# A hybrid attention layer on one core: the first head group's outputs are split earlier, and the feed-forward's transposes are asked for a quarter sooner

## The chip, the core and the metric

The kernel runs on one core of a Trainium2 chip. The core has five engines with their own instruction streams: TensorE (PE; its weight loads are shown as PEld), VectorE (DVE), ScalarE (ACT), GpSimd (POOL) and SyncE (SP), which here issues all DMAs. Each engine takes its instructions in the order that the built program gives them, and waits on semaphores where an instruction needs another engine's or a DMA's result. The metric is the device time of one execution in microseconds (us), less is better.

## What is computed

One layer of a streaming encoder, for 1024 rows of 1024 numbers in float32, in three parts. Each part's output is RMS-normalised and added to the rows.

```python
h = rmsnorm(x, g_mix_pre);  proj = h @ w_in
y_fox = forgetting_attention(fq, fk, fv, f_logit)          # 8 heads of 64, causal
y_chk = chunked_relpos_attention(cq, ck, cv, rel_bias)     # 8 heads of 64, own chunk + 8 before
y = concatenate([rmsnorm(y_fox, g_fox_out), rmsnorm(y_chk, g_chk_out)])
x = x + rmsnorm(y @ w_out, g_mix_post)
h = rmsnorm(x, g_mem_pre)
y = memory_cross_attention(h, rmsnorm(mem, g_mem_kv), w_mq, w_mk, w_mv, w_mo)   # 4 heads, 256 memory rows
x = x + rmsnorm(y, g_mem_post)
h = rmsnorm(x, g_ff_pre)
y = square(relu(h @ w_ff1)) @ w_ff2
x = x + rmsnorm(y, g_ff_post)
```

## The kernel before

**Numbers in two parts.** Each float32 operand of a product is held as a rounded high part and the rest as a low part (`hi`, `lo`), and a product is three matmuls (`mm3`, lines 102 to 104): high by high, high by low, low by high. A weight tile is loaded into a `wraw` buffer (3 of them, line 87), ACT copies its high part (`whi`, line 96), and DVE or POOL subtracts to get the low part (`wlo`, line 97); there are two buffers each of `whi` and `wlo`. For the weights of the memory, `lo_eng()` picks the engine: DVE and POOL in turn, or DVE alone while the flag `quiet[0]` is set.

**Buffers.** Most activations live in one pool of 31 equal buffers (`u4`). PSUM has pairs of banks under the tags `mm`, `s`, `tr` and `pv`.

**Stages.** After the projections, `attend` runs the sixteen heads two by two, in the order `("c",0) ("c",1) ("f",0) ("f",1) ("f",2) ("f",3) ("c",2) ("c",3)`; "f" are the forgetting heads, "c" the chunked ones. So the forgetting heads are all done before the last two pairs of chunked ones. Each head's result goes to a DRAM tile `od[k][half]` (line 396). Beside the last heads the memory is normalised and transposed (`mem_turn`), and its keys are made: `mem_side(mT, "w_mk", "km")` gives eight tiles of 24 matmuls (`mkm`), and `fold_keys` multiplies them with `w_mq` in advance (`fk`, sixteen results of twelve matmuls, evacuated into `fks` and stored as `wk`). Then the pool `p1` of attention is closed and `p2` opened in its place.

Next come `gpost` and `gmem` (two gain rows spread over all partitions), `head_outputs` for both halves of the rows and group 0 (the forgetting heads): it loads `od` back into `oin` (line 570), multiplies by the group's gain and splits into `yT_hi` (ACT, line 573) and `yT_lo` (DVE, line 574), and sums the squares into `sq` (lines 577 to 582). `mem_side(mT, "w_mv", "vm")` makes the memory's values, again eight tiles (`mvm`). `mix_out` is the output projection (`yw`); its `head_rstd` turns `sq` into the inverse norms with four one-column matmuls a half (`ssh`, line 589). `close_block` adds the residual row (`xth`, line 670) and norms it.

After the cross attention (`cross`, `ms`), `mem_out` makes its output for each half (`ym`). For the second half it takes a function that it calls after each quarter `kp` of the weights:

```python
def meanwhile(kp):
    if kp in (0, 2):
        turn(y0, 0, h3[0], "h3", PAIRS[kp // 2:kp // 2 + 1])
    second_weights(kp)
```

`turn` transposes two row tiles of the first half for the feed-forward (`tr_h`, line 127, evacuated into `h3T`, lines 140 and 141). The feed-forward follows.

**What sets the order.** Where `tc.manual_schedule()` is open (the value projections at the start, and everything from the second half's last output tiles on) the engines take the instructions as written. Everywhere else, and so in all that the change touches, the build places each instruction by its own reckoning of times, earlier-written work first where both could go. The order is then fixed in the program; on the chip nothing overtakes on an engine.

Of the kernel before, what the change touches and what calls it, by code (L numbers as in the profile page):

```python
# [33 lines left out]
def f(ap):  # L34
    return ap.bitcast(F32)


def layer(tc, out, t):
    nc = tc.nc
    ctx = ExitStack()  # L40
    with ctx:
        build(ctx, tc, nc, out, t)


def build(ctx, tc, nc, out, t):
    def pool(name, bufs=1, space=None, stack=ctx, **kw):
        if space is not None:
            kw["space"] = space
        return stack.enter_context(tc.tile_pool(name=name, bufs=bufs, reuse_waits="tile", **kw))
# [9 lines left out]
    def mm_tile(shape, name, tag="mm"):  # L59
        return psp.tile(shape, F32, tag=tag, bufs=2, name=name)  # L60

    def u4(name, shape, dt=F32R):

        return up.tile(list(shape), dt, tag="u4", bufs=31, name=name)
# [18 lines left out]
    def load_w(src, shape, alloc=None, lo_on=None):  # L83
        n = wcount[0]
        wcount[0] += 1
        raw = wp.tile(shape, F32, tag="wraw", bufs=3, name=f"wraw{n}")
        nc.sync.dma_start(raw, src)
        return split_w(raw, shape, n, alloc, lo_on)
# [11 lines left out]
    def mm3(ps, lh, ll, rh, rl, start, stop, more=False):  # L100

        nc.tensor.matmul(ps, lh, rh, start=start, stop=False, skip_group_check=more)  # L102
        nc.tensor.matmul(ps, lh, rl, start=False, stop=False, skip_group_check=more)  # L103
        nc.tensor.matmul(ps, ll, rh, start=False, stop=stop, skip_group_check=more)  # L104
# [15 lines left out]
    def to_T(xa, xb, act, c0, name, tags=("tr", "tr")):  # L120

        trs = [mm_tile([P, 2, 2, P], f"tr_{name}_{k}", tags[k // 4]) for k in range(0, KC, 2)]

        def turn(k, q):
            xn = (xa, xb)[q]
            for j in range(2):
                nc.tensor.transpose(trs[k // 2][:, j, q, :], xn[:, (k + j) * P:(k + j + 1) * P], ident)

        ahead = tags[0] != tags[1]
        if ahead:  # L130
            for k in range(0, KC, 2):
                turn(k, 0)
        for k in range(0, KC, 2):
            if not ahead:
                turn(k, 0)
            turn(k, 1)
            src = trs[k // 2].rearrange("p a q b -> p a (q b)")
            i, o = k // act.per, k % act.per
            dh = act.h[i][:, o:o + 2, c0:c0 + 256]
            nc.scalar.activation(dh, src, AF.Copy)  # L140
            nc.vector.tensor_sub(act.l[i][:, o:o + 2, c0:c0 + 256], src, f(dh))  # L141
# [32 lines left out]
    p1s = ExitStack()  # L174
# [240 lines left out]
    def mem_turn():  # L415
        mT = Act("mT", NM)
        xs = [raw_tile(f"memn{b}") for b in range(2)]
        for b in range(2):
            nc.sync.dma_start(xs[b], md[b])
        to_T(*xs, mT, 0, "mem")  # L420
        return mT

    flip = [0]
    quiet = [False]

    def lo_eng():
        flip[0] ^= 1
        return nc.vector if flip[0] or quiet[0] else nc.gpsimd

    def row_pair(w, kp, nh):  # L430
        return w[kp * 2 * P:(kp + 1) * 2 * P, nh * HT:(nh + 1) * HT].rearrange(
            "(a p) n -> p a n", p=P)

    def mem_side(mT, src, name):

        act = Act(name, NM)
        for nb in range(KC):
            wh, wl = load_w(t[src][nb], [P, KC, P], lo_on=lo_eng())
            ps = mm_tile([P, NM], f"m{name}{nb}")
            for kc in range(KC):  # L440
                mm3(ps, wh[:, kc, :], wl[:, kc, :], mT.hi(kc), mT.lo(kc), kc == 0, kc == KC - 1)
            nc.scalar.activation(act.hi(nb), ps, AF.Copy)
            nc.vector.tensor_sub(act.lo(nb), ps, f(act.hi(nb)))
        return act

    def fold_keys(km):

        for h in range(4):
            for mh in range(2):
                wh, wl = load_w(row_pair(t["w_mqT"], h, mh), [P, 2, HT], lo_on=lo_eng())  # L450
                for kp in range(2):
                    ps = mm_tile([P, 2, NM], f"fk{h}{mh}{kp}")
                    for a in range(2):
                        c = slice((kp * 2 + a) * P, (kp * 2 + a + 1) * P)
                        for d in range(2):
                            mm3(ps[:, a, :], wh[:, d, c], wl[:, d, c], km.hi(h * 2 + d), km.lo(h * 2 + d),
                                d == 0, d == 1)
                    g = u4(f"fks{h}{mh}{kp}", (P, 2, NM), F32)
                    if kp:
                        nc.vector.tensor_scalar(g, ps, 0.0625, None, op0=ALU.mult)  # L460
                    else:
                        nc.scalar.activation(g, ps, AF.Copy, scale=0.0625)
                    nc.sync.dma_start(kd_d[mh * 2 + kp][h // 2][:, :, h % 2 * NM:(h % 2 + 1) * NM], g)
# [67 lines left out]
    for n, (kind, pr) in enumerate(order):  # L531
# [10 lines left out]
        for a in range(2):  # L542
# [5 lines left out]
            if a == 0 and n == 6:  # L548
                mT = mem_turn()
        ops = nxt  # L550
    fold_keys(mem_side(mT, "w_mk", "km"))
    p1s.close()


    quiet[0] = True
    p2s = ExitStack()
    p2 = pool("p2", stack=p2s)
    p2xs = ExitStack()
    p2x = pool("p2x", stack=p2xs)

    def head_outputs(th, g):

        yh = [u4(f"yT_hi{th}{g}{i}", (P, 2, HT)) for i in range(2)]
        yl = [u4(f"yT_lo{th}{g}{i}", (P, 2, HT)) for i in range(2)]
        sq = u4(f"sq{th}{g}", (P, HT), F32)
        for i in range(2):
            o = u4(f"oin{th}{g}{i}", (P, 2, HT), F32)
            for j in range(2):
                kc = g * 4 + i * 2 + j
                nc.sync.dma_start(o[:, j, :], od[kc][th])  # L570
                gc = gcol[:, kc:kc + 1]
                dh = yh[i][:, j, :]
                nc.scalar.activation(dh, o[:, j, :], AF.Copy, scale=gc)
                nc.vector.scalar_tensor_tensor(yl[i][:, j, :], o[:, j, :], gc, f(dh),
                                               op0=ALU.mult, op1=ALU.subtract)
            if i == 0:
                nc.scalar.activation(sq, o[:, 0, :], AF.Square)
                nc.scalar.activation(o[:, 1, :], o[:, 1, :], AF.Square)
            else:
                nc.scalar.activation(o, o, AF.Square)  # L580
                nc.vector.tensor_add(sq, sq, o[:, 0, :])
            nc.vector.tensor_add(sq, sq, o[:, 1, :])
        return yh, yl, sq

    def head_rstd(th, g, sq):
        rs = small.tile([P, 4], F32, tag="rs4", bufs=4, name=f"rs{th}{g}")
        ps = mm_tile([P, 4], f"ssh{th}{g}", "pv")
        for b in range(4):
            nc.tensor.matmul(ps[:, b:b + 1], sq[:, b * P:(b + 1) * P], o512, start=True, stop=True)
        nc.vector.tensor_scalar(rs, ps, EPS, None, op0=ALU.add)  # L590
        nc.gpsimd.tensor_tensor(rs, rs, mhalf[:, 0:4], op=ALU.pow)
        return rs
# [5 lines left out]
    def y_tiles(nm, th):  # L598
        return ([u4(f"y{nm}{th}{b}", (P, D), F32) for b in range(4)],
                [small.tile([P, 2], F32, tag="ssy", bufs=8, name=f"ss{nm}{th}{b}") for b in range(4)])  # L600

    PAIRS = ((0, 1), (2, 3))
# [76 lines left out]
    def turn(y, th, act, nm, pairs=PAIRS):  # L679
        for a, b in pairs:  # L680
            to_T(y[a], y[b], act, a * P, f"{nm}{th}{a}")
# [38 lines left out]
    gpost = gain(p2, t["g_mix_post"], "g_mix_post")  # L720
    gmem = gain(p2, t["g_mem_pre"], "g_mem_pre")
    h2, h3 = [], []
    parts = {(th, 0): head_outputs(th, 0) for th in range(2)}
    quiet[0] = False
    vm = mem_side(mT, "w_mv", "vm")
    quiet[0] = True
    ys = [y_tiles("w", th) for th in range(2)]
    mix_out((0, 1), 0)
    for th in range(2):
        parts[th, 1] = head_outputs(th, 1)  # L730
# [23 lines left out]
    def second_weights(kp):  # L754
        if kp == 3:
            wo.extend(load_w(vd_d[k][1], [P, 2, HT], u4, lo_eng()) for k in range(4))
# [7 lines left out]
    h3 = [Act("h3T0")]  # L764
    y0, o = y, o1
# [118 lines left out]
    xf, wo = {}, []  # L884

    def meanwhile(kp):
        if kp in (0, 2):
            turn(y0, 0, h3[0], "h3", PAIRS[kp // 2:kp // 2 + 1])
        second_weights(kp)

    mem_out(1, o, y, ss, gmpost, (0,), meanwhile)
    for i in range(4):
        for a in range(2):
# [530 lines left out]
```

## Time and profile before

Three runs took 1562.92, 1563.53 and 1563.54 us; the median is 1563.53.

| | |
|---|---|
| profiled execution, its own time | 1564.92 us |
| its span | 1562.8 us |
| mean granted TensorE clock | 0.988 |
| PE busy | 1502.7 us (96%), 7948 instructions |
| DVE busy | 940.7 us (60%) |
| ACT busy | 795.9 us (51%) |
| POOL busy | 386.6 us (25%) |
| chain that ended last: PE / DVE / issue / ACT / DMA | 82% / 6% / 3% / 3% / 3% |
| DMA | 237.49 MB, mean 152 GB/s |

Shares of the span. A matmul's busy time is longer than the distance to the next, since matmuls overlap, so a busy PE is read together with the starts of its instructions. In a timeline line the columns are start, duration, engine, line, operation, output and inputs; the bracket at its end is the engine's idle time just before and what ended it. A line of SPq is a DMA being issued, not the transfer.

### The profile page before, as it was taken

Reading aid. Unit: us, or ns where it says so; the run is one execution under the profiler, and the core shown is the slowest. Engines: PE = TensorE matmul, PEld = TensorE weight load, DVE = VectorE, ACT = ScalarE, POOL = GpSimd, SP = SyncE. Lnnn points to the kernel's source line nnn. Section 1 sums busy time; section 2 is a strip of 40 time slices with the busy share of each in tenths; the row PEclk is TensorE's granted clock in tenths of the full one; section 3 lists DMA queues with packets and bytes.
Section 4 is the critical chain, followed back from the end, with each engine's and each line's share of the span. In section 5 each row is a group of like instructions: output and inputs, shape, how many; then the busy total and the mean of one; then the engine's idle time right before and its main releaser. Section 6 shows DMA issues by size and latency. Waiting matters only on the chain.

```text
span 1562.8 us, 22218 instructions
## 1 busy us (share of the span) xinstructions
PE 1502.7 (96%) x7948; PEld 1277.9 (82%) x7948; DVE 940.7 (60%) x1608; ACT 795.9 (51%) x1409; POOL 386.6 (25%) x550
## 2 busy tenths in 40 slices
PE   8999999999999967999999989999999999999998
PEld 7978889789878967776888877888888888888886
DVE  6366574755476743368655568666555574846577
ACT  5356564665466744555454345554555444444442
POOL 4234341343233531002220240433323100000011
PEclk9999999999999998999999999999999999999999
DMA  5132231242223483157523453775444495535565
GB/s 212 50 94 65 60 104 32 81 131 64 55 68 102 144 285 113 68 202 269 197 86 114 156 176 114 253 258 197 153 156 148 166 399 203 171 100 194 208 241 190
DMA packets 90640, 237.49 MB, mean 152 GB/s; under 512 B 10505, under 2 KB 18705, under 8 KB 90530
## 3 DMA queue, kind: packets, MB, share of 16 engines
q1 hardware_dynamic: 90530, 236.08, 45.3%
q8 instruction: 63, 1.03, 0.3%
q14 instruction: 47, 0.39, 0.1%
HBM read 168.35 MB, written 59.30 MB: 146 GB/s over the span
## 4 chain that ended last, share of the span: by engine, by line
PE 82%; DVE 6%; issue 3%; ACT 3%; DMA 3%; POOL 2%; SPq 0%; DVEq 0%; POOLq 0%; ACTq 0%
PE fx L103 4%; PE fx L104 3%; PE fx L102 3%; PE fy L102 3%; PE fy L104 3%; PE fy L103 3%; PE px L104 3%; PE px L102 3%; PE px L103 3%; PE v L104 2%; PE v L102 2%; PE v L103 2%; PE ms L104 2%; PE ms L102 2%; PE ms L103 2%
## 5 line engine op out<-in xcount | busy, mean ns | idle before, releaser
L96 ACT ACTIVATE whi<-wraw 128x1024 fp32r<-128x1024 f32 x92 | 96.8, 1057 | 97.8 <-PE ms L104 29.2
L97 DVE TENSOR_TENSOR wlo<-wraw,whi 128x1024 fp32r<-128x1024 f32 x64 | 79.2, 1243 | 78.4 <-ACT whi L96 78.3
L1151 ACT ACTIVATE whif<-ra 128x1024 fp32r<-128x1024 f32 x37 | 39.2, 1060 | 122.5 <-PE fy L103 62.6
L1153 DVE TENSOR_TENSOR wlof<-ra,whif 128x1024 fp32r<-128x1024 f32 x37 | 45.3, 1225 | 91.2 <-ACT whif L1151 91.2
L1267 POOL TENSOR_SCALAR rf<-sf 128x1 f32<-128x1 f32 x8 | 8.3, 1034 | 326.4 <-ACT jf L1252 326.2
L97 POOL TENSOR_TENSOR wlo<-wraw,whi 128x1024 fp32r<-128x1024 f32 x28 | 67.3, 2405 | 63.6 <-ACT whi L96 42.3
L102 PE MATMUL v<-whiv,hT_hi 128*128 128x256 f32 (+1 forms) x256 | 73.2, 286 | 1.5 <-DVE vs L238 1.5
L104 PE MATMUL v<-whiv,hT_lo 128*128 128x256 f32 (+1 forms) x256 | 73.0, 285 | 0.2 <-DVE hT_lo L141 0.2
L103 PE MATMUL v<-wlov,hT_hi 128*128 128x256 f32 (+1 forms) x256 | 73.1, 286 | 0.0
L104 PE MATMUL fx<-vhif,wlof 128*128 128x512 f32 x168 | 65.4, 389 | 0.0
L102 PE MATMUL fx<-vhif,whif 128*128 128x512 f32 x168 | 65.4, 389 | 0.0
L103 PE MATMUL fx<-vlof,whif 128*128 128x512 f32 x168 | 65.4, 389 | 0.0
L1041 POOL TENSOR_TENSOR sc<-wf,wf 128x512 f32<-128x512 f32 x14 | 22.1, 1579 | 143.4 <-DMA wf<-in_w_ff 117.7
L102 PE MATMUL yw<-whi,yT_hi 128*128 128x512 f32 x128 | 50.3, 397 | 3.4 <-ACT yw L626 1.9
L102 PE MATMUL ym<-whi,oT_hi 128*128 128x512 f32 x128 | 49.8, 404 | 3.0 <-DVE h3T_lo L141 3.0
L103 PE MATMUL yw<-wlo,yT_hi 128*128 128x512 f32 x128 | 50.3, 393 | 1.7 <-DVE wlo L97 1.7
L103 PE MATMUL ym<-wlo,oT_hi 128*128 128x512 f32 x128 | 51.1, 399 | 0.0
L104 PE MATMUL ym<-whi,oT_lo 128*128 128x512 f32 x128 | 51.0, 398 | 0.0
L103 PE MATMUL ms<-wlo,h2T_hi 128*128 128x512 f32 x128 | 50.4, 394 | 0.0
L102 PEld LDWEIGHTS v<-whiv,hT_hi 128*128 128x128 f32 x256 | 48.7, 190 | 1.9 <-DVE vs L238 1.7
L104 PE MATMUL yw<-whi,yT_lo 128*128 128x512 f32 x128 | 49.9, 390 | 0.0
L104 PE MATMUL ms<-whi,h2T_lo 128*128 128x512 f32 x128 | 49.9, 394 | 0.0
(752 smaller groups left out, 5160.9 us busy)
## 6 DMA issues: line engine op xcount, KB each, us to landing
ra<-gd SPq DMA_DIRECT2D x56, 512.0 KB, 3.8
wg<-in_w_ff SPq DMA_DIRECT2D x56, 512.0 KB, 5.8
wf<-in_w_ff SPq DMA_DIRECT2D x38, 512.0 KB, 3.8
gd<-s SPq DMA_DIRECT2D x48, 256.0 KB, 2.1
wraw<-in_w_qk SPq DMA_DIRECT2D x16, 512.0 KB, 3.5
wraw<-wk SPq DMA_DIRECT2D x16, 512.0 KB, 3.5
wraw<-wv SPq DMA_DIRECT2D x16, 512.0 KB, 3.5
gd<-u SPq DMA_DIRECT2D x32, 256.0 KB, 2.4
```

The costliest lines, as they stand in the source:

```text
L96: nc.scalar.activation(hi, raw, AF.Copy)
L97: (lo_on or nc.gpsimd).tensor_sub(lo, raw, f(hi))
L102: nc.tensor.matmul(ps, lh, rh, start=start, stop=False, skip_group_check=more)
L103: nc.tensor.matmul(ps, lh, rl, start=False, stop=False, skip_group_check=more)
L104: nc.tensor.matmul(ps, ll, rh, start=False, stop=stop, skip_group_check=more)
L1041: eng.tensor_sub(sc[:, k1], r0[:, k0], r1[:, k0])
L1151: nc.scalar.activation(ah, ra, AF.Copy)
L1153: nc.vector.tensor_sub(al, ra, f(ah))
L1267: nc.gpsimd.tensor_scalar(r, ssf[b][:, 0:1], ssf[b][:, 1:2], EPS, op0=ALU.add, op1=ALU.add)
```

## The change

Three things in the text of the program:

- `head_outputs` and its call for group 0 (`parts`) stand before `fold_keys(mem_side(mT, "w_mk", "km"))`, so ahead of the keys and of the closing of `p1`; they stood after the two gains, ahead of `vm`.
- `quiet[0]` isn't lowered around `vm` any more, so `lo_eng()` gives DVE for all of its eight weight splits; four of them were POOL's.
- `meanwhile` asks for the second pair of transposes after the second quarter of the weights, where it was the third.

The number of matmuls, transfers and bytes is the same.

```diff
         ops = nxt
-    fold_keys(mem_side(mT, "w_mk", "km"))
-    p1s.close()
-
-
-    quiet[0] = True
-    p2s = ExitStack()
-    p2 = pool("p2", stack=p2s)
-    p2xs = ExitStack()
-    p2x = pool("p2x", stack=p2xs)
-
     def head_outputs(th, g):
...
         return yh, yl, sq
+
+    parts = {(th, 0): head_outputs(th, 0) for th in range(2)}
+    fold_keys(mem_side(mT, "w_mk", "km"))
+    p1s.close()
+
+
+    quiet[0] = True
+    p2s = ExitStack()
+    p2 = pool("p2", stack=p2s)
+    p2xs = ExitStack()
+    p2x = pool("p2x", stack=p2xs)
...
     h2, h3 = [], []
-    parts = {(th, 0): head_outputs(th, 0) for th in range(2)}
-    quiet[0] = False
     vm = mem_side(mT, "w_mv", "vm")
-    quiet[0] = True
...
     def meanwhile(kp):
-        if kp in (0, 2):
-            turn(y0, 0, h3[0], "h3", PAIRS[kp // 2:kp // 2 + 1])
+        if kp < 2:
+            turn(y0, 0, h3[0], "h3", PAIRS[kp:kp + 1])
         second_weights(kp)
```

## The prediction

> **What bounds the kernel now.** I read the page first: TensorE (PE) is busy for 96% of the span and carries 82% of the chain that ended last, so the kernel is bound by PE wherever PE has work, and a change pays only where PE waits. Next the chain in order of time, which shows one long wait: from 566 us it leaves PE for the loads of `wraw` and `oin` (11.5 us in one piece) and comes back at about 594. Then a table of stretches, with columns of length and then busy time (with count) of PE, PEld, DVE, ACT and POOL, the granted clock, the DMA share and GB/s:
>
> ```profile
> core 0: us, PE busy (x) PEld busy (x) DVE busy (x) ACT busy (x) POOL busy (x), PEclk, DMA share, GB/s
> 493.70:513.75 20.05, 19.93 (x163) 19.32 (x162) 13.34 (x39) 14.13 (x32) 10.43 (x19) 1.00 0.44 148
> 513.75:567.10 53.35, 53.35 (x445) 53.26 (x445) 38.22 (x94) 37.16 (x73) 24.22 (x43) 1.00 0.60 186
> ...
> 573.75:594.54 20.79, 1.87 (x8) 1.78 (x9) 10.36 (x15) 10.27 (x17) 3.32 (x2) 0.61 0.69 243
> ...
> 567.10:616.20 49.10, 28.79 (x211) 27.89 (x210) 19.64 (x28) 19.74 (x29) 11.99 (x6) 0.79 0.57 186
> ```
>
> The first two rows are the last heads of attention: PE full, ACT and DVE two thirds full. The last is the stage of the memory's values (`vm`, eight tiles of 24 matmuls), and the row above it the hole within it. The timeline says whose hole it is; PE, ACT, then SP's queue:
>
> ```profile
> 573.45 0.28 PE L104 MATMUL mvm<-mT_hi,wlo 128*128 128x256 f32 x1
> 591.41 1.87 PE L589 MATMUL ssh<-o,sq 128*128 128x1 f32 x8 [17.68 <-DVE sq L582]
> 594.54 0.58 PE L102 MATMUL mvm<-mT_hi,whi 128*128 128x256 f32 x1 [1.26 <-DVE vm_lo L443]
> ```
> ```profile
> 586.10 1.39 ACT L573 ACTIVATE yT_hi<-oin,gcol 128x512 fp32r<-128x512 f32 x2 [9.01 <-DMA oin<-od]
> ```
> ```profile
> 568.86 1.28 SPq L570 DMA_DIRECT2D oin<-od  x2
> 570.19 0.47 SPq L179 DMA_DIRECT2D g_mix_post<-in_g_mix_post  x1
> 570.70 0.50 SPq L179 DMA_DIRECT2D g_mem_pre<-in_g_mem_pre  x1
> 571.58 0.33 SPq L670 DMA_DIRECT2D xth<-in_x  x1
> ...
> 574.55 1.23 SPq L570 DMA_DIRECT2D oin<-od  x2
> ```
>
> The small matmuls `ssh` stand in PE's fixed order ahead of the third `mvm` tile. They wait for `sq`, that for ACT, that for `oin`, whose loads left in a burst with two gains, two rows of x and the weights.
>
> **Gain: the hole closes.** I compared the fixed order of instructions that each build gives every engine. In the changed one the eight `oin` loads stand some fifty places earlier in SP's queue, among the loads of `w_mk`, and both `ssh` groups among the fold of the keys; between the eight `mvm` tiles nothing foreign is left. A full-speed `mvm` matmul starts every 0.12 us (573.33 to 573.45), so the stage costs 8 x 24 x 0.12 = 23.0 us, where it took 49.0 (567.11 to the first `yw` at 616.13). The difference contains the hole, 1.9 us of slow clock after it (20 matmuls 0.213 us apart) and some 1.3 us at two tiles split on POOL (2.40 us each). The flag for those splits is not lowered any more, so all go to DVE at 1.23 us; with ACT's 1.06 that is 2.3 us, less than the 2.9 of a tile, and PE hides it.
>
> The two gains and two rows of x now stand before the third `mvm` weight in SP's queue. That weight can be issued about 2 us before the stage starts (its buffer is freed by the last POOL split of the keys) and must land by 3.4 us into it (two tiles, 5.8, less the split). It has 5.4 us; loads of weights in the burst took 5.3 in the median, `xth` 10.0. So a wait of 0 to 4.6 us; I take 0.7, by the row of its own kind. Stage: 23.7, a gain of 25.3. The 8 `ssh` columns, which were inside the 49.0, are now outside: 0.95 us (their row at full clock, 602.29) back.
>
> **Cost: the work moves onto full engines.** What moves is 14 ACT operations (8 `yT_hi`, 6 squares: 10.05 us in their rows) and 14 of DVE (8 `yT_lo`, 5.74 us; 6 additions to `sq`, 0.69 each). The built order puts nearly all of it in the stretch 493.70 to 513.75, and ahead of the evacuation of `mkm0` and `mkm1`. Those two tiles hold both `mm` banks, so `mkm2` cannot start: in before, PE filled this stretch with 94 `mkm` matmuls, of which 22 finish the first pair; the other 72 (8.6 us) now stand after it. PE waits in the stretch and does that work later, where it was full. ACT's load there becomes 14.13 + 9.0 (one square falls later) - 2.8 (two weight splits and two evacuations that go with the 72) = 20.3 us; DVE's 13.34 + 5.74 + 2.8 - 2.1 = 19.8. Both fill a stretch that took 20.05, and they feed each other. How tightly they pack is bounded by rows: in 300 to 305 both are busy 4.9 of 5 us, in 445 to 465 about 0.8. So 20.3/0.97 = 20.9 to 20.3/0.80 = 25.4 us, and I take 0.9, between, 22.5. Loss: 2.5 + 8.6 = 11.1 (9.5 to 14.0). It cannot be nothing unless PE finds other work, and its order has none. What is left over (one square, two additions) hides in the 53.35 us that follow, with ACT at 70%. For thinner cover later and stray idle I add 1.3 (0 to 4).
>
> The eight `oin` issues take SP some 0.62 us each and push five loads of `w_mk`, a bias row and four stores of `od` back, 1.2 us a pair. They hide behind the same closed banks. Ten `u4` buffers are held some 80 us longer; `fks` tiles then reuse one seven stores back, 7 x 1.44 us of fold against a store that lands in 4.0, so no wait.
>
> The Trainium skill, "TensorE: Matmul & The Clock Gate" (Part 1), speaks against the move: an idle window of about 3.4 us puts PE at half rate until it has been busy as long. This trace agrees at 594.54 (0.213 us against 0.12 after the hole). If the stretch's idle came in one such piece it would add an estimated 1.7 us (half of 3.4) and make the time 1553.2; in bits it adds none, and the sum is without it.
>
> **The second edit does nothing.** Moving the second pair of transposes from the third quarter to the second of `mem_out` could end PE's wait before `ym11`:
>
> ```profile
> 910.01 0.66 PE L127 MATMUL tr_h<-ident,ym 128*128 128x128 f32 x4 [0.99 <-DVE h3T_lo L141]
> 913.65 0.80 PE L102 MATMUL ym<-whi,oT_hi 128*128 128x512 f32 x1 [2.98 <-DVE h3T_lo L141]
> ```
>
> That is 4.0 us of idle and 13 matmuls at 0.427 us for 0.227, 2.6 more: 6.6 at most. In the other direction, if PE came to them before the last row is normed (893.6), it would lose some 4. But this region is ordered by a scheduler's own reckoning, and from the last `mvm` on the built order of all five engines is the same, instruction for instruction. So 0: the wait at 913.65 stays.
>
> **Sum.** -25.3 + 0.95 + 11.1 + 1.3 = -12.0 us. The profiled execution took 1564.92 us (span 1562.8, 2.1 around it), 1.4 above the median of 1563.53. 1564.92 - 12.0 = 1552.9, against the median 1551.5. The likeliest case's own range, with the bounds above, is 1548.5 to 1558.
>
> **Rivals.**
> - *The burst takes the place of the hole.* The third weight lands after 10.0 us as `xth` did: 4.6 instead of 0.7, and 1.9 us of slow clock. For it: the DMA share of 1.00 in 567 to 574. Against: the eight `oin` loads (2 MB) are out of the burst. 1551.5 + 3.9 + 1.9 = 1557.3.
> - *ACT stands still under the heads: slower.* ACT takes its work in order, so each `yT_hi` whose load is late stops the attention behind it. The loads come in four pairs, and the order leaves each some 3 us; if they take the 7.7 us that they took in the burst, 4 x 4.7 = 19 us are added: 1570. It decides from 3 us a pair (12.0/4). For: the last pair stands in SP's queue behind a load that waits for a POOL split. Against: the DMA share is 0.44 there, and weights in 485 to 515 landed in 3.5 us.
> - *The moved work hides wholly.* PE finds its 8.6 us under the heads and the packing costs nothing: -25.3 + 0.95, 1539. Against: PE is in order, and `mkm2` waits for the banks.
> - *Gain and cost cancel.* The packing falls to 0.6 (20.3/0.6 = 34 us in place of 22.5): -12.0 + 11.5, 1563. Nothing in the trace is as loose as that.
>
> **How the numbers follow.** Forecast 0.60, burst 0.18, slower 0.10, hidden wholly 0.08, cancelled 0.04. The range, 1544 to 1562, holds the forecast, the burst and what lies between the forecast and full hiding; it leaves out the slower case, the far end of full hiding and the cancelled one. A measurement of this kernel can tell about 0.2% (3.1 us) from no change. Faster by more: 0.60 + 0.08 + 0.15 of the burst's 0.18 = 0.83; within: 0.07; slower: 0.10.
>
> **What would show it.** Right: no `ssh` wait on `sq` over 1 us; the eight `mvm` tiles in about 24 us at clock 1.00; PE idle of 8 to 13 us in the c5 head with ACT or DVE near full, and `mkm2` released by an evacuation; the wait before `ym11` still some 3 us. Wrong: PE still full in that head (the cost is too high), `yT_hi` waiting for `oin` by more than 3 us a pair (too low), a wait over 4 us for `wraw` at the third `mvm` tile, or a changed stretch at 910.

## The result, and the profile after

Five runs each on one chip: before 1563.01 us in the median (1562.63 to 1563.54), after 1554.26 us (1553.09 to 1559.4). The ratio is 0.995, with a 95% interval of 0.9933 to 0.9966: faster by 8.8 us. The profiled execution of after has a span of 1552.2 us against 1562.8, 10.6 less, at a granted clock of 0.993 (0.988).

The table of stretches of after answers to the one shown of before. Its columns are the stretch and its length, then the busy time and count of PE, PEld, DVE, ACT and POOL, the granted clock, the DMA share and GB/s. The three rows are the c5 head, the heads and the fold that follow, and the eight tiles of the values:

```profile
492.99:515.11 22.12, 16.42 (x92) 14.10 (x90) 19.98 (x44) 19.18 (x42) 9.46 (x17) 0.79 0.55 188
515.11:580.10 64.99, 64.13 (x531) 63.84 (x532) 43.03 (x105) 41.44 (x78) 29.05 (x46) 0.99 0.54 166
580.10:606.20 26.10, 23.55 (x194) 23.14 (x193) 12.83 (x16) 10.45 (x15) 0.00 (x0) 1.00 0.74 258
```

The values' stage was 49.0 us and is 26.1. The c5 head was 20.05 us with 163 matmul records, and is 22.12 with 92: the 71 that are missing stand in the second row, which grew from 445 to 531 (the eight `ssh` are in it too). DVE and ACT are busy for 19.98 and 19.18 of 22.12 us. The stage of the values starts 13.0 us later (580.10 for 567.10; this execution was 0.7 us ahead at the first `sc5g`, 465.6 for 466.3), and the first `yw` 9.9 us earlier (606.2 for 616.1).

The timeline of after's PE in the three places, each line with start, duration, engine, line, operation, and in brackets the idle time before it and what ended it:

```profile
501.80 0.36 PE L389 MATMUL pvc5g<-phc5g,vs 128*128 128x256 f32 x1 [1.36 <-ACT phc5g L383]
504.75 0.36 PE L390 MATMUL pvc5g<-plc5g,vs 128*128 128x256 f32 x1 [2.59 <-DVE plc5g L384]
...
515.42 0.57 PE L102 MATMUL mkm<-mT_hi,whi 128*128 128x256 f32 x1 [0.39 <-DVE km_lo L443]
...
587.81 0.39 PE L102 MATMUL mvm<-mT_hi,whi 128*128 128x256 f32 x1 [1.79 <-ACT whi L96]
589.07 0.39 PE L104 MATMUL mvm<-mT_hi,wlo 128*128 128x256 f32 x1 [0.76 <-DVE wlo L97]
```

PE stands in pieces under the c5 head; `mkm2` is let go at 515.42 by an evacuation (`km_lo`). `ssh` has no wait any more. The third tile of the values waits 1.79 + 0.76 us for its weight. What that weight waited for, on ACT and in SP's queue of after:

```profile
586.70 1.06 ACT L96 ACTIVATE whi<-wraw 128x1024 fp32r<-128x1024 f32 x1 [3.14 <-DMA wraw<-in_w_mv]
```
```profile
573.25 0.45 SPq L179 DMA_DIRECT2D g_mix_post<-in_g_mix_post  x1
...
574.37 0.72 SPq L179 DMA_DIRECT2D g_mem_pre<-in_g_mem_pre  x1
575.18 1.07 SPq L671 DMA_DIRECT2D xth<-in_x  x2
576.34 1.50 SPq L463 DMA_DIRECT2D wk<-fks  x2
577.94 1.89 SPq L87 DMA_DIRECT2D wraw<-in_w_mv  x2
```

Its load leaves at 577.94 behind two gains, two rows of x and some stores of `wk`, and ACT can start on it at 586.70, 8.8 us later.

### The profile page after: what moved, and what is told of

Read it like the earlier page. It is cut to its first block, busy times and chain, and to the rows that moved or that the text cites. A ratio compares the mean times of both kernels' runs of the same rounds, so it can differ in the third digit from the quotient of the medians.

```text
span 1552.2 us, 22221 instructions
## 1 busy us (share of the span) xinstructions
PE 1504.1 (97%) x7948; PEld 1276.3 (82%) x7948; DVE 946.2 (61%) x1612; ACT 796.5 (51%) x1409; POOL 379.6 (24%) x546
## 3 DMA queue, kind: packets, MB, share of 16 engines
q8 instruction: 63, 1.03, 0.3%
## 4 chain that ended last, share of the span: by engine, by line
PE 84%; DVE 6%; ACT 3%; DMA 3%; issue 2%; POOL 2%; SPq 0%; DVEq 0%; POOLq 0%; ACTq 0%
PE fx L103 4%; PE fx L104 4%; PE fx L102 3%; PE fy L104 3%; PE fy L103 3%; PE fy L102 3%; PE px L104 3%; PE px L103 3%; PE px L102 3%; PE ms L104 2%; PE ms L103 2%; PE ms L102 2%; PE v L102 2%; PE pz L103 2%; PE pz L104 2%
## 5 line engine op out<-in xcount | busy, mean ns | idle before, releaser
L97 DVE TENSOR_TENSOR wlo<-wraw,whi 128x1024 fp32r<-128x1024 f32 x68 | 84.3, 1244 | 75.0 <-ACT whi L96 74.5
L97 POOL TENSOR_TENSOR wlo<-wraw,whi 128x1024 fp32r<-128x1024 f32 x24 | 58.1, 2422 | 48.0 <-ACT whi L96 26.9
```

What stands on the lines that cost most here:

```text
L97: (lo_on or nc.gpsimd).tensor_sub(lo, raw, f(hi))
```

## The experiments

Each kernel was timed in five rounds beside before on the same chip; ratios are to before, with 95% intervals.

**The second edit alone** (before, with the transposes asked for a quarter sooner).

```diff
-        if kp in (0, 2):
-            turn(y0, 0, h3[0], "h3", PAIRS[kp // 2:kp // 2 + 1])
+        if kp < 2:
+            turn(y0, 0, h3[0], "h3", PAIRS[kp:kp + 1])
```

> The kernel before with the second edit alone (second pair of transposes after the second quarter). Theory: the built order of all engines is that of before, so nothing happens: 1563 us within 1.5, and the wait before ym11 stays 2.98 us. Rival (the edit moves the transposes): that wait and the slow clock behind it shrink, 1556 to 1560.

1563.34 us, ratio 0.9999 (0.999 to 1.0007). PE's line before `ym11` in it has the same wait as before and after:

```profile
911.62 0.55 PE L102 MATMUL ym<-whi,oT_hi 128*128 128x512 f32 x1 [2.98 <-DVE h3T_lo L141]
```

The second edit does nothing; all of the 8.8 us is the first's.

**The first edit without its move** (after, with the group read and split behind the fold of the keys; of the first edit only the splits' engine is left).

```diff
-    parts = {(th, 0): head_outputs(th, 0) for th in range(2)}
     fold_keys(mem_side(mT, "w_mk", "km"))
+    parts = {(th, 0): head_outputs(th, 0) for th in range(2)}
```

> The first edit without its move: the first group's outputs are read and split after the fold of the keys, where they stood, and only the splits of the values' weights go to VectorE instead of GpSimd. Theory (the gain is the hole's, the flag is worth the two POOL splits on the path, 1.3 us): 1562.2 us, 1560 to 1564, with a wait of ssh for sq of 10 us or more between the values' tiles. Rival (GpSimd's splits held up the weights' loads, and the flag closed the hole): 1545 to 1553, no such wait.

1560.99 us, ratio 0.9985 (0.9976 to 0.9994). The hole is there, on PE:

```profile
590.97 1.87 PE L590 MATMUL ssh<-o,sq 128*128 128x1 f32 x8 [16.59 <-DVE sq L572]
```

So the splits' engine gives some 2.3 us (0.9 to 3.8 by the interval), and the move the rest. The group here is written just ahead of the two gains, where before had it behind them; the first `oin` pair leaves ahead of the gains in both.

**The values' splits back on GpSimd, in after.**

```diff
+    quiet[0] = False
     vm = mem_side(mT, "w_mv", "vm")
+    quiet[0] = True
```

> The changed kernel with the splits of the values' weights put back on GpSimd where its turn comes (four of the eight tiles), everything else as changed. Theory (a tile of 2.9 us hides 1.06 of ACT and 1.23 of VectorE but not 1.06 and 2.40 of GpSimd, so each of the four tiles waits 0.5 to 0.65 us): a stage longer by 2.0 to 2.6 us, 1555.5 to 1558 us. Rival 1 (the weights stand early enough that GpSimd hides too): within 0.6 us of the changed kernel. Rival 2 (GpSimd frees the buffers later and the next loads leave later): 4 us or more over the changed kernel, with waits for wraw.

1554.41 us, ratio 0.9947 (0.9934 to 0.9961); after, on the same chip: 1553.68. The waits for POOL's splits appear, but three of 0.43 us (1.3 in all), and the waits for the third weight are 1.03 + 0.76 where they were 2.12 + 0.76 in after's execution on this chip. The stage is 27.4 us where that execution had 26.4, so it is longer by 1.0 and not by the theory's 2.0 or more; the 0.7 between the medians is inside the intervals.

**After once more.**

> The changed kernel once more, unedited, so that the other runs of this row stand beside it on the same chip. If its scatter (1553.1 to 1559.4 in the first result) is its own and not the first chip's: a median of 1553 to 1556, a ratio to before of 0.993 to 0.997, and runs spread over more than 3 us. If the scatter was the chip's: the same median, runs within 1.5 us.

1553.68 us (1552.47 to 1554.55), ratio 0.9937 (0.9923 to 0.995). The runs lay within 2.1 us, between what the two expectations said; the run of 1559.4 in the first result did not come again.

**The keys' tiles ahead of the moved work.** If the closed banks make the loss, opening them first should give it back; if the load of ACT and DVE makes it, nothing should change.

```diff
+    km = mem_side(mT, "w_mk", "km")
     parts = {(th, 0): head_outputs(th, 0) for th in range(2)}
-    fold_keys(mem_side(mT, "w_mk", "km"))
+    fold_keys(km)
```

> The changed kernel with head_outputs written after the eight mkm tiles and ahead of the fold. Theory (most of the cost is PE work shut out by the two closed mm banks): mkm2 is back at its old place, PE is full in the stretch of head c5, the 8.6 us of put-off matmuls and the half clock are gone, and the same ACT and DVE work costs 0 to 3 us later: 1543 to 1548. Rival (the load on ACT and DVE costs the same wherever it lies): 1552 to 1556.

1548.35 us, ratio 0.9904 (0.9891 to 0.9917): 0.35 us above the theory's range, and well clear of the rival. Its stretches:

```profile
500.00:520.00 20.00, 20.00 (x163) 19.60 (x164) 13.19 (x36) 11.78 (x27) 9.06 (x16) 1.00 0.47 153
520.00:550.00 30.00, 26.94 (x204) 24.70 (x203) 28.17 (x64) 28.10 (x55) 15.90 (x22) 1.00 0.61 190
```

PE is full under the c5 head. The same work now stands under the c6 head, where DVE and ACT are busy 28.2 and 28.1 of 30 us, and PE's idle there is 3.1 us in bits under 1 us. The values' stage starts at 574.8 instead of 580.1: of the 13.0 us some 5 came from the closed banks.

**The burst behind the values' tiles, in after.** The two gains are written behind `vm`, and a copy of one column of the last tile into each target makes them and the first two rows of x wait for it.

```diff
+            if nm == "h2" and tb < 2:
+                nc.vector.tensor_copy(xt[:, 0:1], f(vm.hi(7, slice(0, 1))))
             nc.sync.dma_start(xt, xin(tb))
...
+        nc.vector.tensor_copy(g[:, 0:1], f(vm.hi(7, slice(0, 1))))
+        nc.sync.dma_start(g, src.to_broadcast([P, D]))
```

> The changed kernel with the two gains and the first two rows of x loaded only when the last vm tile is done (a one-column copy from it into each destination ahead of its load). Theory (the third mvm weight was late because 2 MB stood ahead of it): no wait for wraw at mvm2, the stage of eight tiles 23.5 instead of 26.1 us, 1551 to 1553. Rival (it was late by its own issue): stage 26, 1554; or the late rows of x make close_block wait, above 1555.

1551.48 us, ratio 0.9923 (0.991 to 0.9936). The stage is what 192 matmuls at 0.12 us come to:

```profile
579.30:602.20 22.90, 22.90 (x193) 22.90 (x192) 12.84 (x16) 10.38 (x15) 0.00 (x0) 1.00 0.68 223
```

That the gains' and rows' loads made the third weight late is shown: with them gone from there it leaves 2.2 us ahead of the stage, as in after, lands 4.1 us later, and no `mvm` waits. The stage is 3.2 us shorter. The whole time's gain over after is 2 to 4 us by the ratios, and there the intervals overlap.

**Both placings together.**

> Both better placings in one kernel: the tiles of the keys opened before the moved work, and the two gains and the first two rows of x loaded only behind the last tile of the memory's values. Theory (each edit takes away a wait of its own, and the first has already taken most of the second's: with the keys first the waits for the weight in the values' stage were 1.05 us against 2.55 in the changed kernel): 1547.3 us, 1545.5 to 1548.5, the values' stage 23.0 us. Rival 1 (the gains add up: 5.9 and 2.8 off 1554.3): 1545.6 or less. Rival 2 (the late loads are now the last thing before the first rows are normed, and PE waits there): 1549 or more, with a wait at the first transposes of h2.

1545.9 us, ratio 0.9886 (0.9872 to 0.9899): inside the theory's range, but 1.4 us under its price and 0.3 above rival 1, so that these runs don't tell whether the second edit's gain is the smaller for the first. The values' stage takes 23.2 us (574.1 to 597.3), with no wait in it. Against after on the same chip (1553.68) it is 7.8 us less. It beats both kernels.

**What is left under the c6 head.** On top of both placings: first a kernel that leaves out four squares and six additions, then one that leaves nothing out and issues squares later.

```diff
                 nc.scalar.activation(sq, o[:, 0, :], AF.Square)
+            if g == 0:
+                continue
...
```

> The kernel with keys first and late loads, with four of the six squares of the moved first group (3.38 us of ScalarE by their rows: twice 0.63, twice 1.06) and its six additions (4.1 us of VectorE) left out, so that the norm of the first group is taken from a quarter of its values. What is left of the price of the move there is 2.83 us of PE idle in 520 to 550, where ScalarE is busy 27.50 of 30 us and VectorE 28.64. Theory (PE waits because the two are full): with some 3 to 4 us less work on each, PE's idle there falls under 1 us and the time to 1543 to 1544.5 us. Rival (each wait is the length of a chain from score to weight, whatever the load): 1545.2 to 1546.8 us, idle still over 2 us.

```diff
...
     vm = mem_side(mT, "w_mv", "vm")
+    for th in range(2):
+        early[th][3]()
...
```

> The kernel with keys first and late loads, with the same six squares issued after the values' tiles in the code, nothing left out. The built order lets three of them go ahead under the heads as before and moves two squares of 0.63 us and the sums behind the heads, where ScalarE is half idle. Theory (the load under the c6 head is the price): about half of the 2.83 us of idle goes, 1544 to 1545.3 us. Rival (the order of the rest decides, or the sums are late for ssh): 1545.5 us or more.

1543.77 us, ratio 0.9879 (0.9864 to 0.9894), and 1544.33 us, 0.9879 (0.9862 to 0.9895). The row of 520 to 550, first of the kernel with both placings, then of the one without the squares, then of the one with squares later:

```profile
520.00:550.00 30.00, 27.17 (x206) 24.95 (x205) 28.64 (x67) 27.50 (x55) 16.09 (x23) 1.00 0.60 190
```
```profile
520.00:550.00 30.00, 28.57 (x225) 26.99 (x224) 26.30 (x70) 26.98 (x55) 15.72 (x24) 1.00 0.66 203
```
```profile
520.00:550.00 30.00, 27.73 (x218) 26.23 (x217) 26.99 (x66) 28.42 (x57) 15.04 (x24) 1.00 0.66 205
```

With the work gone idle fell by half, from 2.83 to 1.43 us, not to under 1 as the theory had it and not to over 2 as the rival; 19 more matmul records fit in. With squares issued later it fell only to 2.27, where about half was expected to go. Both times agree with the theories, but their intervals overlap with that of both placings alone, so a price of 1 to 2 us for the load is possible and not settled.

**The wait before `ym11`.** It stayed in after, so its cause was tried: the output tiles that follow use the banks which the late transposes hold. Swapping the two pairs of banks, first in after, then on top of both placings:

```diff
-                tr = mm_tile([P, 2, 2, P], f"trx{a}{kp}", ("tr", "pv")[self.i])
+                tr = mm_tile([P, 2, 2, P], f"trx{a}{kp}", ("pv", "tr")[self.i])
...
-        ps = row_tile(o, b, wo, f"ym11{b}", "tr" if b < 2 else "pv")
+        ps = row_tile(o, b, wo, f"ym11{b}", "pv" if b < 2 else "tr")
```

> The changed kernel with the PSUM tags of the last output tiles exchanged (ym110, ym111 in pv and the other two in tr, and the feed-forward's turns the other way round). Theory (ym110 waits for the tr banks that the second pair of transposes holds until their last subtraction): the 2.98 us wait goes, with most of the slow clock after it, 1548 to 1552. Rival (the next thing, row sums or POOL, is late instead): 1554, with the wait under another name.

> The kernel with keys first and late loads, and the banks of the last output tiles and of the transposes swapped as well. Theory (the wait before ym11 is only moved on, as the swap alone showed): 1545 to 1547 us, the same as without the swap. Rival (the swap alone was masked by a chance wait for a weight in the values' stage): 1540 to 1543.5 us.

1555.36 us, ratio 0.9944 (0.9932 to 0.9957), against after's 0.995 and 0.9937; and 1544.38 us, 0.9883 (0.9868 to 0.9897), against 0.9886. The wait is gone (the `ym` stage took 91.9 us from first to last start, after 98.6) and nothing is won: the stage of the transposes `trx` behind it took 32.6 us in place of 25.9. PE's groups in the later half of the kernel, first of after, then with the swap alone, show where it went (count, busy and mean ns, then the idle before them):

```profile
L102 PE MATMUL ym<-whi,oT_hi 128*128 128x512 f32 x128 | 49.6, 402 | 3.0 <-DVE h3T_lo L141 3.0
...
L104 PE MATMUL px<-h3T_hi,wlo_a 128*128 128x512 f32 x24 | 9.6, 401 | 0.6 <-DVE wlo_a L827 0.5
```
```profile
L102 PE MATMUL ym<-whi,oT_hi 128*128 128x512 f32 x128 | 48.5, 394 | 0.0
...
L104 PE MATMUL px<-h3T_hi,wlo_a 128*128 128x512 f32 x24 | 10.6, 441 | 3.1 <-DVE wlo_a L827 3.1
```

PE comes earlier to the feed-forward's first weights and waits there 3.1 us for their split on DVE, where it had waited 0.6. The granted clock of the 8 us behind that wait (950 to 958) was 0.68, so the slow matmuls came back as well.

**All of the keys' splits on VectorE, in after.** PE's longest idle under the c5 head in after, 2.59 us, ended with a DVE operation behind one `yT_lo` of 2.78 us, where the others took 0.73 to 1.09.

```diff
+    quiet[0] = True
     parts = {(th, 0): head_outputs(th, 0) for th in range(2)}
```

> The changed kernel with all sixteen splits of the keys' weights on VectorE, where every second one was GpSimd's; nothing left out. In the changed kernel one yT_lo of VectorE took 2.78 us where its median is 0.75: it began beside a GpSimd split (500.26 to 503.00) and ended 0.55 us after it, and PE's longest idle of the stretch, 2.59 us, ended with what stood behind it. Theory (a VectorE operation that reads two tiles in SBUF stands until GpSimd's is over): no yT_lo of the group over 1.2 us, PE's longest idle in the stretch under 1.5 us; VectorE has 2.0 us less of standing and 1.23 of one more split, so the time falls by 0.5 to 2 us, to 1552 to 1553.5, and less of the stretch is at half clock. Rival 1 (the long yT_lo waits for its own data and GpSimd stands beside it by chance): it stays over 2 us. Rival 2 (the standing goes, but the splits fill VectorE, which sets the stretch): no long yT_lo, and the time at 1554 us or more.

1553.77 us, ratio 0.9952 (0.9938 to 0.9965). Under the heads the theory is right: the longest `yT_lo` is 1.00 us, PE's longest idle in the stretch 1.34, and the values' stage starts at 578.1, 2.0 us earlier than in after. The time is that of rival 2 all the same, no better than after's by the ratio (0.995 and 0.9937), but it came about in another way. The values' stage is now 28.3 us; PE, then ACT:

```profile
585.22 0.39 PE L102 MATMUL mvm<-mT_hi,whi 128*128 128x256 f32 x1 [1.24 <-DVE vm_lo L443]
589.43 0.39 PE L102 MATMUL mvm<-mT_hi,whi 128*128 128x256 f32 x1 [1.08 <-ACT whi L96]
590.69 0.39 PE L104 MATMUL mvm<-mT_hi,wlo 128*128 128x256 f32 x1 [0.76 <-DVE wlo L97]
```
```profile
582.51 1.06 ACT L96 ACTIVATE whi<-wraw 128x1024 fp32r<-128x1024 f32 x1 [3.31 <-DMA wraw<-in_w_mv]
```

PE comes to the stage sooner, and the burst of loads is still there: two weights are waited for instead of one. ACT stood 3.31 us for the third weight before it evacuated the first tile, so the third tile waited for its bank (`vm_lo`), and the fourth tile waited for its own weight. Some 15 matmuls after that start 0.21 us apart. What was won under the heads was lost here.

## Why the prediction came out as it did

It said 1551.5 us, 12.0 less than before; measured were 8.8 (first result) and 10.0 less (after once more), and 10.6 in the spans. The direction and the mechanism were right, and a term of the sum was too good. By the trace the change is worth 9.2 us at the first `yw`: the stage of the values is 22.9 us shorter, for 25.3, and starts 13.7 later, for 13.35.

- *The hole closes.* Right: no `ssh` waits, and nothing foreign stands between the tiles. Undoing the move alone brought back a wait of 16.59 us.
- *The third weight's wait, 0.7 us.* This is the term that was mis-sized, and a row was misread for it. The 5.3 us are the median of this row of before (540 to 600):

```profile
wraw<-in_w_mv SPq DMA_DIRECT2D x7, 512.0 KB, 5.3
```
```profile
572.00 0.82 SPq L87 DMA_DIRECT2D wraw<-in_w_mv  x1
573.73 0.77 SPq L87 DMA_DIRECT2D wraw<-in_w_mv  x1
```

  The row mixes loads that left ahead of the burst (3.9 and 5.2 us at 555.74 and 557.54) with these two, which left inside it and landed after 10.8 and 11.7 us: no faster than `xth` (10.0), from which the first rival made 4.6. Besides, 5.3 us fit into the 5.4 that were reckoned, so the 0.7 followed from no row. In after the load took 8.8 us from its issue to ACT's start. It was issued 2.2 us before the stage, as the working had it (about 2), and PE waited 2.55 us (2.88 in the second execution of after), inside the bounds of 0 to 4.6. The stage cost 26.1 us instead of 23.7; with the burst put behind it, 22.9. The rival's 1.9 us of slow clock did not come in after (clock 1.00).
- *The loss under the c5 head, 11.1 us, and 1.3 + 0.95 behind it.* Right in sum, and partly by luck: the stage of the values started 13.0 us later, 13.7 when the 0.7 by which this execution was ahead is added, for 13.35. The stretch was 22.1 us for 22.5, 71 matmuls were put off for 72, and DVE and ACT packed at 0.90 and 0.87 for the 0.9 that was chosen. But that 0.9 was a choice between two bounds, ACT had 19.2 us of work and not 20.3, and of DVE's 20.0 us some 2.0 were no work but standing (last section), which no term held.
- *Why that loss.* The closed banks were named as its larger part (8.6 of 11.1). The runs bear them out, at a smaller size: opened first, they gave 5.3 us back at the start of the stage. The load then costs under the c6 head what it no longer costs under the c5 head.
- *The clock in the stretch, left out of the sum.* The row of before that bore on it was the pace after the hole. In after the granted clock fell in the stretch itself:

```profile
500.00:505.00 5.00, 1.05 (x5) 0.48 (x5) 4.94 (x5) 4.07 (x11) 2.84 (x2) 1.00 0.37 126
505.00:510.00 5.00, 4.14 (x19) 3.23 (x18) 4.51 (x13) 4.60 (x10) 1.57 (x4) 0.56 0.70 236
510.00:515.00 5.00, 4.60 (x19) 4.24 (x19) 5.00 (x13) 4.58 (x12) 2.60 (x4) 0.50 0.02 3
```

  PE was busy 1.05 of 5 us, with idle pieces of 1.36 and 2.59 and one matmul between them, and then had about half its clock for 10 us. "In bits it adds none" was wrong as to the clock; the stretch was no longer than forecast all the same. That DVE and ACT set its length, busy for 4.5 to 5.0 of every 5 us there, is the likely reason and was not tried by itself. From 516 the matmuls were 0.12 us apart again. The Trainium skill, "TensorE: Matmul & The Clock Gate" (Part 1, in its section on a second failure mode), says that frequent short idles between groups of matmuls suffice to throttle the clock; these rows agree.
- *The rival in which ACT stands still for `oin`.* It did not come: ACT's only wait for those loads under the heads was 1.19 us.
- *The second edit.* Right: nothing, and the wait of 2.98 us unchanged. Its worth, put at up to 6.6 us, is not there to be had: with the wait taken away the feed-forward's first weights are late instead.
- *The likeliest case's own range, 1548.5 to 1558.* By the bounds named beside it the sum gives 1548.0 to 1557.2 with a wait of 0 to 0.7 us at the third weight, and up to 1561 with one of 4.6. The measured medians lie inside either way.

## What to carry to other kernels

When work is moved under a full engine, look for what it is put ahead of: here the evacuation of two tiles, which kept PE's banks closed and cost some five of the thirteen microseconds lost, and issuing the tiles first won half as much again as the whole change had, or more. A transfer in a burst should be priced by those transfers that left inside that burst, not by a median over quieter ones too, and whatever isn't needed yet sent behind it. A wait that is removed is worth at most the slack of the next thing on that engine, so read on in the timeline to the next weight.

## What the runs showed of the hardware

One thing was not expected, though the trace of before had it already. An operation of VectorE that reads two tiles in SBUF stands still when it meets a GpSimd split that is already running. In before, GpSimd's split of a weight and an addition of `sq` which otherwise took 0.69 us; first POOL, then DVE:

```profile
576.65 2.34 POOL L97 TENSOR_TENSOR wlo<-wraw,whi 128x1024 fp32r<-128x1024 f32 x1 [5.87 <-ACT whi L96]
```
```profile
577.12 2.42 DVE L582 TENSOR_TENSOR sq<-sq,oin 128x512 f32<-128x512 f32 x1 [1.19 <-ACT oin L578]
```

The addition ended 0.55 us after the split (579.54 and 578.99), nearly as if it had begun when the split was done. In after a `yT_lo` beside a split (500.77 for 2.78 us, the split until 503.00) did the same, also with 0.55 us; with the splits off GpSimd no `yT_lo` took over 1.00. The other order can be seen in the kernel with the keys first: a split that began 0.10 us after a `yT_lo` showed 3.56 us where its mean in after is 2.42, and the `yT_lo` (533.61) and the addition behind it took their usual 0.74 and 0.66.

```profile
533.71 3.56 POOL L97 TENSOR_TENSOR wlo<-wraw,whi 128x1024 fp32r<-128x1024 f32 x1 [2.89 <-ACT whi L96]
```

The Trainium skill, "SBUF — State Buffer" ("SBUF: two separate sides"), says that the two engines share one pair of ports as an exclusive lock, which whoever starts first holds for its whole instruction; the two cases with GpSimd first and the one with VectorE first agree. The prediction priced the moved VectorE work by its undisturbed rows; the standing added 2.0 us to VectorE's time under the c5 head, though taking it away did not make the kernel faster.
